# A hybrid encoder layer on one core: norm, sums and transposes behind the last output round given out in steps

## The chip, the cores and the metric

The kernel runs on one core of a Trainium2 chip. The metric is the device time of one execution, in microseconds. The engines are TensorE (PE, with its weight loads shown apart as PEld), VectorE (DVE), ScalarE (ACT), GpSimd (POOL) and SyncE (SP), which issues the transfers.

## The reference

One layer of an encoder trunk on a sequence of 1024 positions with 1024 channels, in float32:

```
h  = RMSNorm(x);  [q|k|v|glu|q_mem] = h @ W_in
A  = dilated sliding-window attention, 8 heads x 64
B  = GLU -> depthwise conv 31 -> LayerNorm -> swish
C  = cross-attention into 256 memory tokens, 4 heads x 64
x  = x + concat(A, B, C) @ W_out
x  = x + ConvFFN(RMSNorm(x))
     ConvFFN: up (1024 -> 2 x 2816) -> depthwise conv 3 -> silu(gate) * up -> down (2816 -> 1024)
```

The change touches what lies between the last two lines: the second RMSNorm, and the way its result gets into the up projection.

## The kernel before

Every matrix product is made in three passes: each operand is split into a high part, rounded to the format that TensorE multiplies quickly, and a low part, the rest, and the products high x high, high x low and low x high are added up. `split` (L1203 on) does it for weights: ScalarE copies the high part (L1207), GpSimd or VectorE subtracts it for the low part (L1208).

The residual lies in eight tiles `x_sb[t]` of 128 positions x 1024 channels. The output projection adds to them in six rounds. In the last round, after the two products of tile t, the generator `norm(t)` is started: `sp.dma_start` stores the row for the end, ScalarE sums the squares, GpSimd makes the inverse root in two instructions (`rsqrt`, L164 and L165), and VectorE scales both halves of the row by it and by the gains (L1173, two instructions).

The up projection isn't made as eight block products, but in the manner of Strassen and Winograd, as seven: the normed rows, transposed, form a two by two block matrix. Its rows of blocks are the tiles 0 to 3 and 4 to 7, its columns the two halves of the channels. The seven left operands are A11, A12 (tiles 0 to 3), A22 (tiles 4 to 7) and the sums S1, S2, S3, S4. For t from 4 on `norm` makes the sums in place, of the rows of tile t and of tile t - 4: `high1` becomes high0 + high1 on GpSimd (L1183), `high0` becomes low0 - high0 on VectorE (L1184), `low0` becomes high1 - low0 on VectorE (L1185), and `low1` becomes low1 - low0 on GpSimd (L1189). `high1` is transposed as A22 before it is overwritten. "Tile 5" below is x_sb[5] with its partner x_sb[1].

`turn_rows` makes one operand's 128 columns: four transposes on TensorE into a PSUM tile `ps_n` (L1159; two buffers, under the tag "turn"), then ScalarE copies the high part out (L1161), then VectorE subtracts for the low part (L1162). `norm` has 24 such turns, two (A11, A12) for each t under 4 and four (A22, S1, S3, S2) for each t from 4 on; four S4 turns follow later. So a turn must wait for a free `ps_n`, which is freed by its second reader.

Then comes the up stage. `first_column` makes the A11 and A12 products of the first two column tiles early, in `ps_a`. `gated(ct)` does one column tile of gate and up (22 rounds): it loads four weight blocks, makes four sums of them t1 to t4 (`comb`, L1221, on VectorE but for the first two rounds), splits seven operands, and runs seven products of 12 matmuls each (128 x 128 by 128 x 512, L1226). The sums of the products are put together as they come: p5 is ScalarE's copy of the S1 product in `ps_c` (L1278); `cu` gets ps_d + p5 on VectorE (L1280, S3 product); u2 is ps_b + p1 (L1283, S2 product); GpSimd adds u2 to the upper half of cu (L1284); the S4 product goes on adding to `ps_c` and L1286 reads it; the A22 product goes on adding to `ps_d` and L1288 reads it. Thus S4 can't start before p5 is read, and A22 not before L1280. Behind them stands the depthwise convolution: ScalarE's scaled copy (L1293) and two VectorE instructions (L1294, L1295) for each of yu and yg, Silu on ScalarE (L1296), and the gate's product (L1297). The down stage (`ps_dn`, L1334) then runs over the stored gate.

The order of the work comes from two places. The program is written with generators: `st.start` hands one over, and each `st.tick()` moves all that are alive by one `yield`; `out_projections` yields after every six matmuls, so that a generator's instructions fall between them. On that written order the framework's scheduler sets the order of each engine's instructions by its own timeline, with priorities. So a change in the written order can change the order of instructions far behind it. Every engine runs its queue strictly in order.

Of the kernel before, what the change touches and what calls it, by code (L numbers as in the profile page):

```python
# [132 lines left out]
def block(tc, a, out):  # L133
# [3 lines left out]
    def f32(ap):  # L137
        return ap.bitcast(F)
# [23 lines left out]
    def rsqrt(dst, src, scale):  # L162

        pool.tensor_scalar(dst, src, scale, EPS, OP.mult, OP.add)  # L164
        pool.tensor_tensor(dst, dst, expo[:, : dst.shape[1]], OP.pow)  # L165
# [989 lines left out]
    def turn_rows(rows, nm, t):  # L1155

        ps = psp.tile([128, KH, 128], F, name="ps_n", tag="turn", bufs=2)
        for k in range(KH):
            pe.transpose(ps[:, k], rows[:, 128 * k : 128 * k + 128], ident)  # L1159
        hi, lo = (x[:, :, 128 * t : 128 * t + 128] for x in ops[nm])  # L1160
        act.activation(hi, ps, AF.Copy)  # L1161
        dve.tensor_tensor(lo, ps, f32(hi), OP.subtract)  # L1162

    def norm(t):
        x = x_sb[t]
        sp.dma_start(h_d[t], x)
        sq = p3r.tile([128, D], F, name="sq2", tag="wide", bufs=2)
        col = ss2[:, t : t + 1]
        act.activation(sq, x, AF.Square, accum_out=col)
        rsqrt(col, col, 1.0 / D)  # L1170
        for i, g in enumerate(g_ffn):
            half = x[:, 512 * i : 512 * i + 512]
            dve.scalar_tensor_tensor(half, half, col, g, OP.mult, OP.mult)  # L1173
        if t < 4:
            turn_rows(x[:, 0:512], "A11", t)
            turn_rows(x[:, 512:1024], "A12", t)
            yield
            return
        yield

        (low0, low1), (high0, high1) = ((y[:, 0:512], y[:, 512:1024]) for y in (x_sb[t - 4], x))
        turn_rows(high1, "A22", t - 4)
        pool.tensor_tensor(high1, high0, high1, OP.add)  # L1183
        dve.tensor_tensor(high0, low0, high0, OP.subtract)  # L1184
        dve.tensor_tensor(low0, high1, low0, OP.subtract)  # L1185
        turn_rows(high1, "S1", t - 4)
        turn_rows(high0, "S3", t - 4)
        turn_rows(low0, "S2", t - 4)
        pool.tensor_tensor(low1, low1, low0, OP.subtract)  # L1189
        yield  # L1190
# [176 lines left out]
```

## Time and profile before

| | us |
|---|---|
| median of 3 runs | 1310.51 (1309.11 to 1313.55) |
| the profiled execution's own time | 1310.28 |
| its span in the trace | 1308.5 |
| mean granted clock of TensorE | 0.963 of full speed |
| busy: TensorE, VectorE, GpSimd, ScalarE | 1197.1, 868.7, 788.5, 626.6 |

About 1.8 us of the profiled time lie outside its span. The stages that matter here: the last round of the output projection with the first products of the up stage ends at about 594.5 us of the span; the transposes go on to about 624.7; the up stage goes on to about 1064, and the down stage to the end. In the lines below a row of an engine's timeline has its start, its duration, engine, line, operation, written tile <- read tiles, shapes, count, and in brackets the idle time before it with what ended it.

### The profile page before, as it was taken

The numbers are of one execution on the slowest core, as the hardware profiler recorded it, in microseconds if no ns is written. First come the engines' busy times: TensorE is split into PE (matmuls) and PEld (weight loads), VectorE is DVE, ScalarE is ACT, GpSimd is POOL, SyncE is SP. The second block draws the span as 40 slices with busy tenths as digits, with TensorE's granted clock in tenths as the row PEclk, the third lists the DMA queues.
The fourth block names the chain that finished last, engine by engine and source line by source line (L and its number), as shares of the span: only waits on it lengthen the run. The fifth ranks groups of instructions, "written<-read, shape, count | busy, mean of one in ns | idle before, by whom it ended". The sixth has DMA issues, their size and how long they took to land.

```text
span 1308.5 us, 18556 instructions
## 1 busy us (share of the span) xinstructions
PE 1197.1 (91%) x6287; PEld 1000.3 (76%) x6287; DVE 868.7 (66%) x1272; ACT 626.6 (48%) x1296; POOL 788.5 (60%) x793
## 2 busy tenths in 40 slices
PE   4899988799988898885999999999999999999997
PEld 3887887799877786563877777777777788888886
DVE  6748879676685786887487778778787762224222
ACT  5664165468766576553344444344444443333331
POOL 4835286498894454367466667676676745555552
PEclk9999988999989898896999999999999999999999
DMA  7353525566575622161122222222222254448443
GB/s 253 112 170 100 159 82 161 169 180 178 144 252 164 188 74 78 28 213 49 34 87 81 65 86 67 81 89 65 89 71 83 81 175 155 145 145 272 146 146 120
DMA packets 166555, 164.81 MB, mean 126 GB/s; under 512 B 20322, under 2 KB 125756, under 8 KB 166460
## 3 DMA queue, kind: packets, MB, share of 16 engines
q1 hardware_dynamic: 166460, 163.63, 40.3%
q8 instruction: 49, 0.80, 0.3%
q14 instruction: 46, 0.38, 0.1%
HBM read 121.51 MB, written 42.08 MB: 125 GB/s over the span
## 4 chain that ended last, share of the span: by engine, by line
PE 46%; DVE 18%; issue 8%; ACT 7%; POOL 6%; DMA 5%; SPq 1%; POOLq 0%; ACTq 0%; DVEq 0%
PE ps_dn L1334 18%; PE ps_c L1226 6%; PE ps_d L1226 6%; PE proj L1099 4%; PE proj L917 3%; DVE yg L1295 3%; DVE conv L980 2%; DVE yu L1295 2%; PE o L287 2%; DMA v<-vr_d 2%; POOL up_lo L1208 2%; PE turn L278 2%; PE ps_a L1226 2%; ACT yu L1293 2%; DVE yg L1294 1%
## 5 line engine op out<-in xcount | busy, mean ns | idle before, releaser
L917 PE MATMUL proj<-w_hi,hnT 128*128 128x256 f32 x896 | 188.1, 298 | 23.7 <-ACT raw L832 12.9
L1208 POOL TENSOR_TENSOR up_lo<-dn_raw,up_hi 128x512 fp32r<-128x512 f32 x88 | 131.7, 1517 | 114.1 <-ACT up_hi L1207 111.3
L1208 POOL TENSOR_TENSOR up_lo<-up_sum,up_hi 128x512 fp32r<-128x512 f32 x88 | 154.8, 1768 | 55.8 <-PE ps_c L1226 22.7
L917 PEld LDWEIGHTS proj<-w_hi,hnT 128*128 128x128 f32 x896 | 150.9, 200 | 27.9 <-ACT raw L832 14.1
L1208 POOL TENSOR_TENSOR up_lo<-up_raw,up_hi 128x512 fp32r<-128x512 f32 x66 | 116.0, 1760 | 68.8 <-PE ps_a L1226 46.3
L1208 DVE TENSOR_TENSOR up_lo<-dn_raw,up_hi 128x512 fp32r<-128x512 f32 x44 | 57.6, 1311 | 147.5 <-ACT up_hi L1207 141.4
L1207 ACT ACTIVATE up_hi<-dn_raw 128x512 fp32r<-128x512 f32 x132 | 75.1, 623 | 161.4 <-issue 118.8
L1334 PE MATMUL ps_dn<-up_lo,up_hi 128*128 128x512 f32 x352 | 136.8, 389 | 0.0
L1334 PE MATMUL ps_dn<-up_hi,up_lo 128*128 128x512 f32 x352 | 136.3, 389 | 0.0
L1334 PE MATMUL ps_dn<-up_hi 128*128 128x512 f32 x352 | 134.7, 389 | 0.0
L917 PE MATMUL proj<-w_lo,hnT 128*128 128x256 f32 x448 | 131.9, 294 | 0.0
L1226 PE MATMUL ps_c<-S,up_hi 128*128 128x512 f32 x352 | 113.5, 404 | 6.6 <-ACT p L1278 6.6
L1226 PE MATMUL ps_a<-A,up_hi 128*128 128x512 f32 x352 | 111.1, 396 | 0.0
L636 POOL TENSOR_TENSOR w_lo<-w_raw,w_hi 128x512 fp32r<-128x512 f32 x44 | 62.8, 1437 | 59.4 <-ACT w_hi L634 58.8
L1221 DVE TENSOR_TENSOR up_sum<-up_raw,up_sum 128x512 f32<-128x512 f32 x40 | 59.0, 1476 | 50.4 <-POOL up_lo L1208 50.4
L917 PEld LDWEIGHTS proj<-w_lo,hnT 128*128 128x128 f32 x448 | 89.7, 200 | 0.5 <-POOL w_lo L624 0.4
L980 DVE SCALAR_TENSOR_TENSOR conv<-conv,cwT 128x1009 f32<-128x1009 f32 (+14 forms) x60 | 89.3, 1488 | 0.8
L1226 PEld LDWEIGHTS ps_c<-S,up_hi 128*128 128x128 f32 x352 | 65.4, 190 | 28.3 <-ACT p L1278 13.6
L1111 DVE TENSOR_TENSOR x<-proj,x 128x512 f32<-128x512 f32 x96 | 64.1, 682 | 25.0 <-PE proj L1099 24.9
L1293 ACT ACTIVATE yu<-cu,fwT 128x1024 f32<-128x1024 f32 x22 | 27.4, 1244 | 108.0 <-DVE cu L1286 106.3
L1226 PEld LDWEIGHTS ps_a<-A,up_hi 128*128 128x128 f32 x352 | 65.8, 188 | 15.8
L1334 PEld LDWEIGHTS ps_dn<-up_lo,up_hi 128*128 128x128 f32 x352 | 66.1, 188 | 13.8
(240 smaller groups left out, 3150.2 us busy)
## 6 DMA issues: line engine op xcount, KB each, us to landing
up_raw<-w_up SPq DMA_DIRECT2D x92, 256.0 KB
dn_raw<-w_down SPq DMA_DIRECT2D x88, 256.0 KB
g_d<-yg SPq DMA_DIRECT2D x22, 512.0 KB
dn_raw<-g_d SPq DMA_DIRECT2D x44, 256.0 KB
x<-x SPq DMA_DIRECT2D x16, 512.0 KB
qk_d<-out SPq DMA_DIRECT2D x32, 256.0 KB
qk<-qk_d SPq DMA_DIRECT2D x16, 512.0 KB
w_raw<-w_in SPq DMA_DIRECT2D x40, 128.0 KB
```

Source lines behind the costliest of these rows:

```text
L636: (dve if next(chunk_no) < EARLY else pool).tensor_tensor(lo, raw, f32(hi), OP.subtract)
L917: pe.matmul(ps[:, :256], lhs[i][:, k], c.parts[k][j], start=(k == 0 and i == 0 and j == 0), stop=(k == KT - 1 and i == 1))
L980: dve.scalar_tensor_tensor(acc[:, c0:c1], conv_in[i][:, c0 + k - 15 : c1 + k - 15], w, acc[:, c0:c1], OP.mult, OP.add)
L1099: pe.matmul(ps, mixed[k][i][:, 128 * t : 128 * t + 128], wo[k, half][j], start=(n == 0), stop=(n == 3 * len(ks) - 1))
L1111: dve.tensor_tensor(dst, ps, dst, OP.add)
L1207: act.activation(hi, src, AF.Copy)
L1208: adder.tensor_tensor(lo, src, f32(hi), OP.subtract)
L1221: adder.tensor_tensor(t, x, y, OP.subtract)
L1226: pe.matmul(ps, w[i][:, k], ops[x][j][:, k], start=(first and n == 0), stop=(n == 3 * KH - 1), skip_group_check=not first)
L1293: act.activation(y, c, AF.Identity, scale=tap[1], bias=b)
L1295: dve.scalar_tensor_tensor(y[:, 0 : S - 1], c[:, 1:S], tap[2], y[:, 0 : S - 1], OP.mult, OP.add)
L1334: pe.matmul(ps, gk[i][:, 128 * t : 128 * t + 128], wk[half][j], start=(k == 0 and m == 0), stop=(k == NF - 1 and m == 2))
```

## The change

In `norm`, `yield`s are added: two after `rsqrt`, three after the scaling, one between the turns of A11 and A12, three after the two VectorE sums, and one behind each of the turns of S1 and S3. One, ahead of the part for t from 4 on, is taken out. A turn of the next tile's products can be written between any two of these steps. No instruction is added or removed.

```
--- before.py
+++ after.py
@@ -1168,23 +1168,31 @@
         col = ss2[:, t : t + 1]
         act.activation(sq, x, AF.Square, accum_out=col)
         rsqrt(col, col, 1.0 / D)
+        for _ in range(2):
+            yield
         for i, g in enumerate(g_ffn):
             half = x[:, 512 * i : 512 * i + 512]
             dve.scalar_tensor_tensor(half, half, col, g, OP.mult, OP.mult)
+        for _ in range(3):
+            yield
         if t < 4:
             turn_rows(x[:, 0:512], "A11", t)
+            yield
             turn_rows(x[:, 512:1024], "A12", t)
             yield
             return
-        yield
 
         (low0, low1), (high0, high1) = ((y[:, 0:512], y[:, 512:1024]) for y in (x_sb[t - 4], x))
         turn_rows(high1, "A22", t - 4)
         pool.tensor_tensor(high1, high0, high1, OP.add)
         dve.tensor_tensor(high0, low0, high0, OP.subtract)
         dve.tensor_tensor(low0, high1, low0, OP.subtract)
+        for _ in range(3):
+            yield
         turn_rows(high1, "S1", t - 4)
+        yield
         turn_rows(high0, "S3", t - 4)
+        yield
         turn_rows(low0, "S2", t - 4)
         pool.tensor_tensor(low1, low1, low0, OP.subtract)
         yield
```

Behind the diff all lines move down by 2 to 8: L1173 is now L1175, L1183 to L1185 are L1187 to L1189, L1189 is L1197, and from L1207 on 8 are added (L1221 is L1229, L1286 is L1294, L1297 is L1305). The order of instructions moves on all engines, from the last output round to the end of the up stage. Three places follow. In the rows x_4988 to x_4995 are the tiles x_sb[0] to x_sb[7], and ss_7000 holds the sums of squares.

GpSimd, from the last inverse root (tile 7) on, before:

```order
L165 TENSOR_TENSOR ss_7000<-ss_7000,expo 128x1
L1189 TENSOR_TENSOR x_4988<-x_4988 128x512
L1208 TENSOR_TENSOR up_lo<-up_sum,up_hi 128x512
L1208 TENSOR_TENSOR up_lo<-up_raw,up_hi 128x512
L1221 TENSOR_TENSOR up_sum<-up_raw 128x512
L1208 TENSOR_TENSOR up_lo<-up_sum,up_hi 128x512
L1221 TENSOR_TENSOR up_sum<-up_raw 128x512
L1221 TENSOR_TENSOR up_sum<-up_raw,up_sum 128x512
L1183 TENSOR_TENSOR x_4993<-x_4993 128x512
L1208 TENSOR_TENSOR up_lo<-up_sum,up_hi 128x512 x2
L1221 TENSOR_TENSOR up_sum<-up_raw,up_sum 128x512
L1208 TENSOR_TENSOR up_lo<-up_sum,up_hi 128x512
```

and after:

```order
L165 TENSOR_TENSOR ss_7000<-ss_7000,expo 128x1
L1187 TENSOR_TENSOR x_4993<-x_4993 128x512
L1197 TENSOR_TENSOR x_4988<-x_4988 128x512
L1216 TENSOR_TENSOR up_lo<-up_sum,up_hi 128x512
L1216 TENSOR_TENSOR up_lo<-up_raw,up_hi 128x512
L1216 TENSOR_TENSOR up_lo<-up_sum,up_hi 128x512
L1229 TENSOR_TENSOR up_sum<-up_raw 128x512 x2
L1197 TENSOR_TENSOR x_4989<-x_4989 128x512
L1187 TENSOR_TENSOR x_4994<-x_4994 128x512
L1229 TENSOR_TENSOR up_sum<-up_raw,up_sum 128x512
L1216 TENSOR_TENSOR up_lo<-up_sum,up_hi 128x512 x2
```

The sum of tile 5 (x_4993) has moved from behind seven instructions to directly behind the inverse root, and the sums of tiles 6 and 7 have come nearer to it, ahead of weight sums and splits that stood before them.

TensorE, from the turn of S2 of tile 4 (it reads x_4988) to the first products of `gated` (ps_d, with the turn of S2 of tile 7, which reads x_4991, and the first S4 turn, which reads x_4988 again, beside them), before:

```order
L1159 MATMUL ps_n<-identr,x_4988 128x128 x4
L1159 MATMUL ps_n<-identr,x_4993 128x128 x12
L1159 MATMUL ps_n<-identr,x_4989 128x128 x4
L1159 MATMUL ps_n<-identr,x_4994 128x128 x12
L1159 MATMUL ps_n<-identr,x_4990 128x128 x4
L1159 MATMUL ps_n<-identr,x_4995 128x128 x12
L1226 MATMUL ps_d<-S_6998,up_hi 128x512 x2
L1159 MATMUL ps_n<-identr,x_4991 128x128 x4
L1159 MATMUL ps_n<-identr,x_4988 128x128 x4
L1226 MATMUL ps_d<-S_6999,up_hi 128x512
```

and after:

```order
L1159 MATMUL ps_n<-identr,x_4994 128x128 x4
L1159 MATMUL ps_n<-identr,x_4988 128x128 x4
L1159 MATMUL ps_n<-identr,x_4993 128x128 x8
L1159 MATMUL ps_n<-identr,x_4995 128x128 x4
L1159 MATMUL ps_n<-identr,x_4989 128x128 x4
L1159 MATMUL ps_n<-identr,x_4994 128x128 x8
L1159 MATMUL ps_n<-identr,x_4990 128x128 x4
L1159 MATMUL ps_n<-identr,x_4995 128x128 x8
L1159 MATMUL ps_n<-identr,x_4991 128x128 x4
L1234 MATMUL ps_d<-S_6998,up_hi 128x512 x2
L1159 MATMUL ps_n<-identr,x_4988 128x128 x4
L1234 MATMUL ps_d<-S_6999,up_hi 128x512
```

Before, the three turns A22, S1 and S3 of a tile stand together (x12). Now A22 of tile 6 comes ahead of S1 of tile 5, and so on; the A22 turn of tile 5 is no longer here, since it stands among the A11 products of `first_column` (17 of them are ahead of it).

VectorE, one round in the middle of the up stage (`up_sum<-up_raw` are t1 and t3, `up_sum<-up_raw,up_sum` t2 and t4), before:

```order
L1280 TENSOR_TENSOR cu<-ps_d,p_9026 128x512
L1221 TENSOR_TENSOR up_sum<-up_raw,up_sum 128x512
L1283 TENSOR_TENSOR u_9027<-ps_b,p_9024 128x512
L1221 TENSOR_TENSOR up_sum<-up_raw,up_sum 128x512
L1286 TENSOR_TENSOR cu<-ps_c,u_9027 128x512
L1294 SCALAR_TENSOR_TENSOR yu<-cu,fwT,yu 128x1023
L1288 TENSOR_TENSOR cg<-ps_d,u_9027 128x512
L1295 SCALAR_TENSOR_TENSOR yu<-cu,fwT,yu 128x1023
L1294 SCALAR_TENSOR_TENSOR yg<-cg,fwT,yg 128x1023
L1295 SCALAR_TENSOR_TENSOR yg<-cg,fwT,yg 128x1023
L1221 TENSOR_TENSOR up_sum<-up_raw 128x512 x2
L1297 TENSOR_TENSOR yg<-yg,yu 128x1024
```

and after:

```order
L1288 TENSOR_TENSOR cu<-ps_d,p_9026 128x512
L1229 TENSOR_TENSOR up_sum<-up_raw,up_sum 128x512
L1291 TENSOR_TENSOR u_9027<-ps_b,p_9024 128x512
L1294 TENSOR_TENSOR cu<-ps_c,u_9027 128x512
L1229 TENSOR_TENSOR up_sum<-up_raw,up_sum 128x512
L1302 SCALAR_TENSOR_TENSOR yu<-cu,fwT,yu 128x1023
L1296 TENSOR_TENSOR cg<-ps_d,u_9027 128x512
L1303 SCALAR_TENSOR_TENSOR yu<-cu,fwT,yu 128x1023
L1302 SCALAR_TENSOR_TENSOR yg<-cg,fwT,yg 128x1023
L1303 SCALAR_TENSOR_TENSOR yg<-cg,fwT,yg 128x1023
L1305 TENSOR_TENSOR yg<-yg,yu 128x1024
L1229 TENSOR_TENSOR up_sum<-up_raw 128x512 x2
```

L1286 (now L1294) has moved ahead of t4, and L1297 (now L1305) ahead of t1 and t3, directly behind L1295 (now L1303). TensorE's products in such a round stand, before, in the order S3, A12, S1, S2, A11 of the round after, S4, A22; now S3, S1, two matmuls of S2, A12, the rest of S2, S4, one matmul of A11 of the round after, A22, the rest of that A11. GpSimd's order within these rounds is the same. On ScalarE Silu is now followed by the split of w1, p5, and the split of w2.

More of the change, by code (lines that the diff above doesn't have):

```diff
@@ L1170, in norm @@
         rsqrt(col, col, 1.0 / D)
+        for _ in range(2):
+            yield
         for i, g in enumerate(g_ffn):
@@ L1173, in norm @@
             dve.scalar_tensor_tensor(half, half, col, g, OP.mult, OP.mult)
+        for _ in range(3):
+            yield
         if t < 4:
             turn_rows(x[:, 0:512], "A11", t)
+            yield
             turn_rows(x[:, 512:1024], "A12", t)
@@ L1178, in norm @@
             return
-        yield
         (low0, low1), (high0, high1) = ((y[:, 0:512], y[:, 512:1024]) for y in (x_sb[t - 4], x))
@@ L1185, in norm @@
         dve.tensor_tensor(low0, high1, low0, OP.subtract)
+        for _ in range(3):
+            yield
         turn_rows(high1, "S1", t - 4)
+        yield
         turn_rows(high0, "S3", t - 4)
+        yield
         turn_rows(low0, "S2", t - 4)
```

## The prediction

> **What bounds the kernel now.** I read the page's shares first, then a table of busy time by stage, then the waits of the two stages that the diff can touch, then the instructions of each engine there.
>
> ```profile
> PE 1197.1 (91%) x6287; PEld 1000.3 (76%) x6287; DVE 868.7 (66%) x1272; ACT 626.6 (48%) x1296; POOL 788.5 (60%) x793
> 594.50:624.70 30.20, 14.72 (x59) 10.79 (x60) 20.33 (x24) 10.14 (x17) 18.62 (x15) 0.56 0.15 44
> 624.70:693.50 68.80, 65.91 (x288) 52.58 (x286) 48.04 (x42) 29.84 (x44) 38.62 (x23) 1.00 0.18 58
> 693.50:754.20 60.70, 60.48 (x251) 47.98 (x251) 47.91 (x39) 26.34 (x40) 41.39 (x26) 0.97 0.25 79
> 754.20:1063.80 309.60, 306.10 (x1284) 238.61 (x1285) 240.19 (x198) 134.18 (x199) 207.31 (x121) 1.00 0.27 85
> 1063.80:1308.50 244.70, 236.94 (x1046) 195.90 (x1044) 73.56 (x63) 72.84 (x127) 125.58 (x84) 0.99 0.49 161
> ```
>
> The columns of a stage are its window and length, then busy time (and count) of PE, PEld, DVE, ACT and POOL, then the granted clock. TensorE is busy for 91% of the span, so only a stage where it idles, or runs under its own pace, has anything to give. The first is 594.5 to 624.7, the stretch of the transposes ("turns"): 14.72 of 30.20 us, at a clock of 0.56. The second hides behind 306.10 of 309.60 us in the up stage: a matmul's modelled end overlaps the next one's start, so pace has to be read from starts. The chain of work that ended last gives them, for the S4 product (12 matmuls into ps_c) of some rounds, and last for the first products of the down stage:
>
> ```profile
> 714.63 2.80 PE ps_c L1226 x12
> 734.23 2.79 PE ps_c L1226 x12
> 754.25 3.07 PE ps_c L1226 x12
> 774.55 3.07 PE ps_c L1226 x12
> 1038.64 3.06 PE ps_c L1226 x12
> 1055.70 2.76 PE ps_dn L1334 x12
> ```
>
> From 714.63 to 734.23 a round of 84 matmuls takes 19.60 us (2.80 for 12: TensorE's own pace). From 754.25 to 1038.64 there are 14 rounds of 20.31 us each. So something else than TensorE sets the rounds there. The waits of 754 to 1064 say what (us in total, times, longest):
>
> ```profile
> ACT yu L1293 <- DVE cu L1286: 89.3, 15, 6.4
> DVE up_sum L1221 <- POOL up_lo L1208: 38.1, 14, 2.7
> DVE yu L1294 <- ACT yu L1293: 20.8, 16, 1.4
> PEld ps_c L1226 <- ACT p L1278: 10.2, 15, 0.7
> PEld ps_d L1226 <- DVE cu L1280: 5.3, 14, 0.4
> ```
>
> TensorE waits briefly twice in each round, for p5 (L1278) and for cu (L1280). The long waits are among the vector engines. One round on VectorE, with the two GpSimd instructions that it waits for:
>
> ```profile
> 1016.06 2.39 DVE L1221 TENSOR_TENSOR up_sum<-up_raw 128x512 f32<-128x512 f32 x2
> 1018.37 2.32 DVE L1297 TENSOR_TENSOR yg<-yg,yu 128x1024 f32<-128x1024 f32 x1
> 1020.61 0.68 DVE L1280 TENSOR_TENSOR cu<-ps_d,p 128x512 f32<-128x512 f32 x1
> 1022.32 0.68 DVE L1283 TENSOR_TENSOR u<-ps_b,p 128x512 f32<-128x512 f32 x1
> 1023.14 1.29 POOL L1284 TENSOR_TENSOR cu<-cu,u 128x512 f32<-128x512 f32 x1 [1.29 <-DVE u L1283]
> 1024.39 1.29 POOL L1208 TENSOR_TENSOR up_lo<-up_sum,up_hi 128x512 fp32r<-128x512 f32 x1
> 1025.72 1.77 DVE L1221 TENSOR_TENSOR up_sum<-up_raw,up_sum 128x512 f32<-128x512 f32 x1 [2.72 <-POOL up_lo L1208]
> 1027.41 0.68 DVE L1286 TENSOR_TENSOR cu<-ps_c,u 128x512 f32<-128x512 f32 x1
> 1029.46 1.28 DVE L1294 SCALAR_TENSOR_TENSOR yu<-cu,fwT,yu 128x1023 f32<-128x1023 f32 x1 [1.38 <-ACT yu L1293]
> 1034.22 2.21 DVE L1295 SCALAR_TENSOR_TENSOR yg<-cg,fwT,yg 128x1023 f32<-128x1023 f32 x1
> 1037.62 1.23 DVE L1297 TENSOR_TENSOR yg<-yg,yu 128x1024 f32<-128x1024 f32 x1 [1.19 <-ACT yg L1296]
> ```
>
> This closes on itself: t1 and t3 at 1016.06, ..., L1283, then GpSimd's L1284 and the low part of w4, then t4 (L1221 at 1025.72, whose buffer that low part was reading), L1286, ScalarE's yu, L1294 to L1295, which ends at 1036.43, when the next round's t1 starts: 20.3 us. L1286 stands behind t4 in VectorE's queue although S4, its input, ended at 1021.4: 6 us lost there, and ScalarE and L1294 wait behind it. The vector loop, not TensorE, is the bound of some 15 rounds.
>
> **The change, part by part.** No instruction is added or removed. Only orders move: in `norm` by the yields, and behind it in the up stage, where the scheduler came out with another order on all engines.
>
> *Turns.* The waits of 545 to 640, with the instructions:
>
> ```profile
> PE ps_n L1159 <- POOL x L1183: 6.8, 2, 5.4
> PE ps_n L1159 <- DVE x L1184: 5.2, 2, 4.5
> 601.51 1.12 PE L1159 MATMUL ps_n<-identr,x 128*128 128x128 f32 x4 [5.42 <-POOL x L1183]
> 607.08 1.09 PE L1159 MATMUL ps_n<-identr,x 128*128 128x128 f32 x4 [4.45 <-DVE x L1184]
> 590.12 0.54 POOL L165 TENSOR_TENSOR ss<-ss,expo 128x1 f32<-128x1 f32 x1
> 600.20 1.26 POOL L1183 TENSOR_TENSOR x<-x 128x512 f32<-128x512 f32 x1
> 601.42 2.53 POOL L1208 TENSOR_TENSOR up_lo<-up_sum,up_hi 128x512 fp32r<-128x512 f32 x2
> 603.90 1.27 POOL L1221 TENSOR_TENSOR up_sum<-up_raw,up_sum 128x512 f32<-128x512 f32 x1
> 605.12 1.27 POOL L1208 TENSOR_TENSOR up_lo<-up_sum,up_hi 128x512 fp32r<-128x512 f32 x1
> 587.10 1.18 DVE L1184 TENSOR_TENSOR x<-x,x 128x512 f32<-128x512 f32 x1
> 601.49 5.44 DVE L1184 TENSOR_TENSOR x<-x,x 128x512 f32<-128x512 f32 x1 [4.04 <-POOL x L1183]
> ```
>
> The sum of tile 5 (L1183) sits on GpSimd at 600.20 behind seven operations for the first weights, and TensorE waits 5.42 us for it. In the new order it stands directly behind L165, so it starts at 590.66: a lead of 9.54 us. Its A22 transposes, which must read the old rows first, go into the A11 products. The turns of neighbouring tiles alternate, so one tile's sums run beside another's turns. What eats the lead is the pair of last rows: the same L1184 takes 1.18 us and, while GpSimd ran four operations in a row, 5.44. A further L1184 starved like that costs 4.26. None gives 9.5 of gain, one 5.3, two 1.0; those are the ends. GpSimd keeps three to six operations in a row behind the sums of tiles 5 and 6, so I take one: **-5.3**.
>
> The Trainium skill, "SBUF — State Buffer", "SBUF: two separate sides", calls the ports that VectorE and GpSimd share an exclusive lock: whichever starts first keeps it for its instruction and the other blocks. The row is harsher: 5.44 us spans all of GpSimd's 2.53 + 1.27 + 1.27, so the loser lost four times over. By the page a blocked L1184 would take one operation more and the gain would be near 9; the row decides.
>
> *Rounds of the up stage.* TensorE's order becomes S3, S1, S2, A12, S4, A22 with A11 of the round after around them. VectorE's moves L1286 ahead of t4 and L1297 directly behind L1295, ahead of t1 and t3. In the loop above that takes away L1286 and the wait for yu (1029.46 less 1027.41: 2.05 us), which now lie beside t4's 1.77. It adds the wait for Silu, which t1 and t3 covered: the row at 1037.62 shows it uncovered, 1.19. So 20.3 - 2.05 + 1.19 = 19.4 us, under TensorE's 19.60: the bound passes to TensorE. From S4's end to the end of the next L1280 I add 0.68 + 1.77 + 6.97 (1029.46 to 1036.43) + 1.19 + 2.32 + 2.39 + 0.68 = 16.0; A22 of the next round starts 19.8 after that S4's end. This lead of nearly 4 us absorbs a loop that is somewhat long: at 20.0, 15 rounds lose 6 and get 4 of it back. p5 stands behind one Silu and one copy on ScalarE, some 4 us ahead of S4 as well. Ends: the loop stays at 20.3 (0), or TensorE's pace everywhere. The latter: 734.23 to 1038.64 is 304.41 us for 15 rounds; 15 x 19.60 = 294.0; **-10.4**, which I take.
>
> *First rounds.* Before 693.5 VectorE is also late once:
>
> ```profile
> PE ps_c L1226 <- ACT p L1278: 2.9, 1, 2.9
> ```
>
> There S4 waits for p5 behind a Silu. In the new order S4 comes 12 matmuls (2.8 us) sooner in its round, the vector work hardly sooner. Between -2.9 (stall gone) and +2.8 (twice as long) I take **+0.5**.
>
> *End of the up stage.* The first 12 products of the down stage stand between the last rounds in both orders (the row at 1055.70, at TensorE's pace), and the last gate (L1297) is stored and loaded again before its use. Bounds -1 and +2.3 (one L1297 late), taken **+0.5**. The down stage (1063.8 on) keeps its order.
>
> Sum: -5.3 - 10.4 + 0.5 + 0.5 = -14.7. The profiled execution took 1310.28 us, 0.23 under the median of the runs (1310.51): **1295.6**, I say 1295.5.
>
> **The rivals.**
> 1. *The vector loop stays the bound.* For it: 19.4 is only 0.2 under 19.60, and L1221 and L1297 cost nearly double beside GpSimd (1.23 against 2.32 for L1297). Against it: the 4 us of lead, and the loop is summed with the dear values. Then only the turns gain: 1310.3 - 5.3 + 1 = 1306.
> 2. *The turns give the lead back, the rounds gain.* Two starved L1184: 1310.3 - 1.0 - 10.4 + 1 = 1300. For it the 5.44; against it that GpSimd itself soon has to wait for VectorE (L1189 needs L1185), which ends any starving.
> 3. *Slower: VectorE blocked behind GpSimd in every round.* Now t4 starts when GpSimd is through; moved behind L1286, it and L1297 may each meet one GpSimd operation more (1.27 each). The loop is then 19.4 + 2.5 = 21.9; 15 rounds lose 2.3 each, less 4 of lead: 30.5 over TensorE's pace where 10.4 are lost now, so 1310.3 + 20.1 - 4.3 = 1326. It decides from a loop of about 21 us, 0.7 over today's. Against it: by the stage's row VectorE is busy 240.19 and GpSimd 207.31 of 309.60 us, 15.8 and 13.6 of a round of 20.3, with much of their waiting for each other counted in it, so both have room in 19.6.
> 4. *Nothing changes*: the lead of the turns is lost and the loop stays: 1310.
>
> **How the numbers follow.** The forecast 0.57, rival 2 0.18, rival 1 0.12, rival 3 0.10, rival 4 0.03. 0.3% is 3.9 us, about what a measurement of this kernel can tell from no change. Faster takes the forecast, rival 2 and half of rival 1 (1306 lies at that edge): 0.81; I say 0.80. Same: the other half and rival 4, 0.09. Slower: rival 3 and a little, 0.11. The forecast's own range is 1289 to 1301 (its turns between 9.5 and 1, first rounds and end between their bounds). The range that holds rivals 1, 2 and 4 and the good end (9.5 + 10.4 + 2.9 = 22.8 under) is 1287 to 1311; it leaves out rival 3.
>
> **What would show it.** Right: S4 to S4 in the chain 19.6 us from about 700 to 1040; no wait of PE for p5 or L1280 in steady rounds; L1294 (now L1302) no longer waiting for yu; VectorE waiting about 1.2 us in each round for Silu; dense products from about 619 instead of 624.7; and no 5.42 wait of ps_n for the sum. Wrong: S4 to S4 still at 20.3 or over, with VectorE's L1221 waiting for GpSimd or L1297 near 3 us; more than one L1184 over 4 us; or a stall over 3 us in the first four rounds.

## The result and the profile after

| | before | after |
|---|---|---|
| median of 6 runs each, us | 1311.87 (1309.11 to 1313.97) | 1296.35 (1292.69 to 1300.54) |
| ratio, with its 95% interval | | 0.9884 [0.9868, 0.9901] |
| span of the profiled execution | 1308.5 | 1290.9 |

The forecast was 1295.5. The two profiles differ by 17.6 us, the ratio is worth 15.2; why the two need not agree stands at the end.

The page of the changed kernel, its busy shares and the chain by engine:

```profile
PE 1190.4 (92%) x6287; PEld 1002.1 (78%) x6287; DVE 829.5 (64%) x1272; ACT 633.0 (49%) x1296; POOL 768.5 (60%) x793
PE 46%; DVE 2%; issue 1%; POOL 0%; DMA 0%; ACT 0%; SPq 0%; POOLq 0%; DVEq 0%; ACTq 0%
```

Two of its stages, the turns and the rounds, with the windows cut where its own stages end:

```profile
594.50:619.00 24.50, 16.89 (x65) 12.31 (x66) 18.78 (x23) 9.09 (x16) 20.70 (x14) 0.58 0.19 54
754.20:1046.00 291.80, 291.80 (x1253) 234.45 (x1252) 198.18 (x192) 139.53 (x196) 178.35 (x117) 1.00 0.27 88
```

TensorE is busy for 16.89 of 24.50 us in the first, still at a clock of 0.58, and for all of the second. VectorE's share of the chain fell from 18% to 2%: no vector instruction stands in the way any more in the rounds. It also has less to do there: over this window the same instructions keep VectorE busy 13.3 us of a round of 19.6 (198.18 of 291.80), where it was 15.8 of 20.3. The chain, S4 of three rounds, the ends of a stretch of 15 rounds among them:

```profile
724.81 2.80 PE ps_c L1234 x12
744.41 2.80 PE ps_c L1234 x12
1018.81 2.80 PE ps_c L1234 x12
```

294.00 us for 15 rounds: 19.60 each. One of the later rounds on VectorE:

```profile
845.25 0.69 DVE L1294 TENSOR_TENSOR cu<-ps_c,u 128x512 f32<-128x512 f32 x1 [2.02 <-PE ps_c L1234]
847.06 0.69 DVE L1229 TENSOR_TENSOR up_sum<-up_raw,up_sum 128x512 f32<-128x512 f32 x1 [1.12 <-POOL up_lo L1216]
847.67 1.28 DVE L1302 SCALAR_TENSOR_TENSOR yu<-cu,fwT,yu 128x1023 f32<-128x1023 f32 x1
855.82 1.23 DVE L1305 TENSOR_TENSOR yg<-yg,yu 128x1024 f32<-128x1024 f32 x1 [1.19 <-ACT yg L1304]
856.97 0.68 DVE L1229 TENSOR_TENSOR up_sum<-up_raw 128x512 f32<-128x512 f32 x1
858.85 0.69 DVE L1229 TENSOR_TENSOR up_sum<-up_raw 128x512 f32<-128x512 f32 x1 [1.20 <-POOL up_lo L1216]
```

And one of the earlier rounds: two S4 sums that follow each other, with t1 and t3 between them, and then the busy times of an earlier and of a later round (the columns are those of the stages above):

```profile
748.01 0.69 DVE L1294 TENSOR_TENSOR cu<-ps_c,u 128x512 f32<-128x512 f32 x1
761.49 3.50 DVE L1229 TENSOR_TENSOR up_sum<-up_raw 128x512 f32<-128x512 f32 x2
767.41 0.69 DVE L1294 TENSOR_TENSOR cu<-ps_c,u 128x512 f32<-128x512 f32 x1
747.28:766.88 19.60, 19.60 (x86) 15.75 (x84) 16.16 (x15) 8.98 (x14) 13.01 (x8) 1.00 0.26 84
845.28:864.88 19.60, 19.60 (x86) 15.75 (x84) 12.65 (x14) 9.32 (x14) 11.97 (x9) 1.00 0.25 81
```

The waits of the whole up stage, 640 to 1046 (us in total, times, longest):

```profile
DVE cu L1294 <- PE ps_c L1234: 27.9, 13, 3.6
PE ps_d L1234 <- DVE cu L1288: 4.4, 2, 3.7
```

The first row of the later round is the change of bound: the S4 sum now waits 2.02 us for TensorE, where it stood behind t4 with its input long ready. This room isn't there from the start. In rounds 4 to 8 the S4 sum doesn't wait for TensorE, and the sums follow each other at 19.40 us (748.01 to 767.41), so VectorE, busy for 16.16 us a round (16.20 in a steady round of before), gains 0.20 on TensorE's 19.60 each time. From round 10 on it waits; it is busy for 12.65 in the later round shown. Silu is uncovered by 1.19 us, as foreseen, and costs nothing. TensorE waits in the up stage only twice, in rounds 2 and 3 (3.7 and 0.7 us). In the turns (545 to 640) the waits for GpSimd's sums are gone, and many short ones for the low parts took their place (the waits again, before and after):

```profile
PE ps_n L1159 <- DVE S L1162: 1.3, 3, 0.8
PE ps_n L1159 <- DVE S L1162: 8.7, 9, 2.2
```

The first S3 product starts at 613.80, where it was 621.81:

```profile
613.80 1.20 PE L1234 MATMUL ps_d<-S,up_hi 128*128 128x512 f32 x2
```

Landmarks that both kernels share, from the starts of TensorE's instructions in the two profiles, give where the 17.6 us come from. The changed order has 11 matmuls of A11 (2.57 us) behind A22 that stood ahead of it; the two rows at A22 are set right for that.

| stretch | before | after | difference | forecast |
|---|---|---|---|---|
| start to the last A12 product of `first_column` | 594.07 | 592.96 | -1.1 | 0 |
| to the first S3 product (the turns) | 27.74 | 20.84 | -6.9 | -5.3 |
| to A22 of round 4 (first rounds) | 95.5 | 94.3 + 2.6 | +1.4 | +0.5 |
| to A22 of round 20 (16 rounds) | 324.3 | 313.6 | -10.7 | -10.4 |
| to the end | 266.96 | 269.24 - 2.57 | -0.3 | +0.5 |

### The profile page after: what moved, and what is told of

Same layout as the page of the kernel before. It is cut to its first block, busy times and chain, and to the rows that moved or that the text cites. A ratio compares the mean times of both kernels' runs of the same rounds, so it can differ in the third digit from the quotient of the medians.

```text
span 1290.9 us, 18539 instructions
## 1 busy us (share of the span) xinstructions
PE 1190.4 (92%) x6287; PEld 1002.1 (78%) x6287; DVE 829.5 (64%) x1272; ACT 633.0 (49%) x1296; POOL 768.5 (60%) x793
## 5 line engine op out<-in xcount | busy, mean ns | idle before, releaser
L1216 POOL TENSOR_TENSOR up_lo<-up_sum,up_hi 128x512 fp32r<-128x512 f32 x88 | 142.5, 1624 | 55.6 <-ACT up_hi L1215 48.6
L1216 POOL TENSOR_TENSOR up_lo<-up_raw,up_hi 128x512 fp32r<-128x512 f32 x66 | 103.7, 1573 | 89.5 <-ACT up_hi L1215 79.0
L1234 PE MATMUL ps_a<-A,up_hi 128*128 128x512 f32 x352 | 114.2, 396 | 0.0
L1234 PE MATMUL ps_c<-S,up_hi 128*128 128x512 f32 x352 | 110.4, 395 | 0.0
L1215 ACT ACTIVATE up_hi<-up_sum 128x512 fp32r<-128x512 f32 x88 | 55.0, 628 | 89.9 <-PE ps_c L1234 43.9
L1342 PEld LDWEIGHTS ps_dn<-up_hi,up_lo 128*128 128x128 f32 x352 | 66.1, 188 | 13.9
L1342 PEld LDWEIGHTS ps_dn<-up_hi 128*128 128x128 f32 x352 | 66.1, 188 | 13.7
```

The lines of the kernel that those rows point to most:

```text
L1215: act.activation(hi, src, AF.Copy)
L1216: adder.tensor_tensor(lo, src, f32(hi), OP.subtract)
L1234: pe.matmul(ps, w[i][:, k], ops[x][j][:, k], start=(first and n == 0), stop=(n == 3 * KH - 1), skip_group_check=not first)
L1342: pe.matmul(ps, gk[i][:, 128 * t : 128 * t + 128], wk[half][j], start=(k == 0 and m == 0), stop=(k == NF - 1 and m == 2))
```

## The experiments

Theory A: two gains that have nothing to do with each other on the chip: shorter turns, and rounds that pass from the vector loop to TensorE because the S4 sum no longer stands behind t4. Its rivals are in the expectations. In the diffs, `behind(key, make)` issues what `make` makes on VectorE behind the recorded instruction `key`, in the queue's order alone; nothing waits for its end. "Stretch" is the one of the table's second row. Each ratio is to the kernel before in the same batch of runs; the medians of before lie between 1311.87 and 1315.62 us, so between batches the ratios count and not the times. In the rows of a pinned kernel the lines are moved again; the tiles tell which is which: `cu<-ps_c` is the S4 sum, "DVE cu L1288" the S3 sum.

**One edit alone.**

```
 # before
         dve.tensor_tensor(low0, high1, low0, OP.subtract)
+        for _ in range(3):
+            yield
         turn_rows(high1, "S1", t - 4)
```

> The kernel before with one of the edits alone: the three yields behind the two VectorE sums of norm. Built, its instructions stand on all engines almost as in the changed kernel (4 of 5297 rows of TensorE differ, 6 of 1141 of VectorE, none of GpSimd), while the kernel with all the other yields and without these three stands as before. Theory A (the time hangs on the two new orders: GpSimd's sum of tile 5 directly behind the inverse root, and VectorE's order in the rounds): 1296 us, the changed kernel's time. Rival (each added yield brings its share, by letting other work in between): a third to a half of the 15 us, 1303 to 1306.

Measured 1298.52 us, ratio 0.9878 [0.984, 0.9916]; stretch 20.86, rounds 19.60, the same two waits in rounds 2 and 3. These three yields are the whole change; on the chip the other edits are worth nothing that can be seen.

**The rounds, with norm untouched.** Three kernels pin VectorE's order in the rounds and leave the turns as they were.

```
 # t4 alone
-        t4 = comb(b21, t2, adder)
+        t4 = behind(("cu", ct - 2), lambda: comb(b21, t2, adder))   # "cu": L1286
 # t1 and t3 alone
-        t1 = comb(b12, b11, adder)
+        t1 = behind(("gate", ct - 3), lambda: comb(b12, b11, adder))   # "gate": L1297
-        t3 = comb(b22, b12, adder)
+        t3 = behind(("gate", ct - 3), lambda: comb(b22, b12, adder))
 # both: all three lines
```

> The kernel before, norm untouched; in the up stage t4 of a round is pinned behind the S4 sum (L1286) of the round two ahead, as in the changed kernel. VectorE's t1 and t3 stay ahead of the gate's product, TensorE keeps the order of before (S3, A12, S1, S2, A11, S4, A22). Theory A (L1286 behind t4 is what makes the vector loop longer than TensorE's round): the loop falls from 20.3 to 18.3, TensorE's 19.6 takes over: S4 to S4 19.60, 10 us less, 1301. Rival B (TensorE's new order, S4 directly behind S2, makes the rounds short, VectorE's order only follows): rounds stay at 20.3, 1311.

> The kernel before, norm untouched; only t1 and t3 of a round are pinned behind the gate's product (L1297), so that VectorE has nothing to do while ScalarE makes Silu; t4 stays ahead of the S4 sum. Theory A: the loop grows by Silu's 1.2 us to 21.5, S4 to S4 21.5, some 15 rounds: +18 us, 1329. Rival B (TensorE's order sets the rounds): 20.3 and 1311.

> The kernel before, norm untouched, with both pins of the two runs above: VectorE's order in the rounds is that of the changed kernel, TensorE's order and the turns are those of before. Theory A: loop 20.3 - 2.05 + 1.2 = 19.4, under 19.6: S4 to S4 19.60, 1301, as with t4 alone. Rival B: 20.3, 1311. Rival C (the loop of 19.4 has no room beside GpSimd, and only TensorE's new order gives VectorE the lead that it needs): between, about 20, 1306.

Measured: t4 alone 1304.32 us, ratio 0.9932 [0.9911, 0.9952]; t1 and t3 alone 1326.06, 1.0085 [1.0055, 1.0115]; both 1308.14, 0.996 [0.9943, 0.9977]. The rounds with t4 alone, by the products into ps_d in the chain (A22 and S3, 24 in a row):

```profile
819.93 5.60 PE ps_d L1226 x24
839.53 5.60 PE ps_d L1226 x24
```

VectorE's S4 sum in the same run:

```profile
839.57 0.69 DVE L1294 TENSOR_TENSOR cu<-ps_c,u 128x512 f32<-128x512 f32 x1 [4.44 <-PE ps_c L1226]
```

With t1 and t3 alone, the starts of A22 on TensorE, then VectorE behind Silu:

```profile
826.21 0.73 PE L1226 MATMUL ps_d<-A,up_hi 128*128 128x512 f32 x2 [1.23 <-DVE cu L1288]
847.34 0.73 PE L1226 MATMUL ps_d<-A,up_hi 128*128 128x512 f32 x2 [1.23 <-DVE cu L1288]
842.02 1.23 DVE L1305 TENSOR_TENSOR yg<-yg,yu 128x1024 f32<-128x1024 f32 x1 [1.19 <-ACT yg L1304]
843.16 3.52 DVE L1221 TENSOR_TENSOR up_sum<-up_raw 128x512 f32<-128x512 f32 x2
```

With both, A22 in the chain:

```profile
823.22 3.08 PE ps_d L1226 x12
843.15 3.08 PE ps_d L1226 x12
```

And t4, then t1 and t3, on VectorE in that run:

```profile
847.05 1.78 DVE L1221 TENSOR_TENSOR up_sum<-up_raw,up_sum 128x512 f32<-128x512 f32 x1 [1.96 <-POOL up_lo L1208]
858.91 3.51 DVE L1221 TENSOR_TENSOR up_sum<-up_raw 128x512 f32<-128x512 f32 x2
```

One instruction moved on VectorE, with TensorE's old order, gives 19.60, and VectorE then waits 4.4 us in every round from round 5 on: rival B (TensorE's order makes the rounds short) falls. The kernel gains less than the rounds do, since its first rounds take 98.9 us (from the first S3 product to A22 of round 4) for 95.5. Moving t1 and t3 alone makes the rounds 21.13 and the kernel slower, so this half of the new order is a loss in itself. It is 0.8 more, where 1.2 was expected: Silu's 1.19 is there, but the gate's product is shorter (1.23 for 2.32), and t2 too (0.67 for 1.18), while t1 and t3 together are longer (3.52 for 2.39). With both, 19.93: not the 19.4 of my sum, and a third of a microsecond over TensorE's pace. Rival C was right for this one.

**TensorE's order on top of both.** The pins above, and the matmuls of the rounds held in the changed kernel's order (A11 and S3 from round 5 on). ScalarE's order in the rounds, not pinned, followed into the changed kernel's as well.

```
 # both pins, and
+    for i in a12: tc.add_manual_dep(i, s2[1].name, ...)        # A12 behind two of S2
+    for i in s2[2:]: tc.add_manual_dep(i, a12[-1].name, ...)
+    tc.add_manual_dep(a11[0], last["S4", ct - 1].name, ...)     # one of A11 behind S4
+    for i in a11[1:]: tc.add_manual_dep(i, last["A22", ct - 1].name, ...)
+    for i in s3: tc.add_manual_dep(i, a11[-1].name, ...)
```

> The kernel with both vector pins (rounds of 19.92 us), and TensorE's order in the rounds pinned besides as in the changed kernel: A12 between the second and third matmul of S2, one A11 matmul between S4 and A22, the other eleven behind A22, S3 behind them. Norm and the turns as before. Theory C (with t1 and t3 behind the gate the loop only fits if TensorE's new order frees the weights' buffers one by one, so that GpSimd's splits are spread and don't meet VectorE's t1 and t3): 19.60, 5 us less than with the two pins alone, 1303. Rival (what is missing lies in ScalarE's or GpSimd's order, or in the turns): 19.9, 1308.

Measured 1308.09 us, ratio 0.9943 [0.9915, 0.9972], the interval too wide to tell it from the run with both. The rounds tell it, by the starts of A22 and by t4, and t1 and t3, on VectorE:

```profile
821.31 0.63 PE L1227 MATMUL ps_d<-A,up_hi 128*128 128x512 f32 x2
840.91 0.63 PE L1227 MATMUL ps_d<-A,up_hi 128*128 128x512 f32 x2
843.81 0.69 DVE L1221 TENSOR_TENSOR up_sum<-up_raw,up_sum 128x512 f32<-128x512 f32 x1 [1.95 <-POOL up_lo L1208]
854.65 3.51 DVE L1221 TENSOR_TENSOR up_sum<-up_raw 128x512 f32<-128x512 f32 x2
```

19.60, so TensorE's order, with ScalarE's, is what the two vector pins lack; which of the two does it isn't told apart, so the part of the rival that names ScalarE stands. The reason that I gave isn't shown: t4 is short now (0.69 for 1.78), but t1 and t3 are as long as with the two pins (3.51), and t2 is longer (1.38 for 0.67). The first rounds lost 2.4 us more here (waits of 1.75 and 3.52 for the S3 sum) and the turns 1.5 (an L1184 of 5.43 us, below), which hides the gain in the total.

**The turns.** First GpSimd's place alone (before, no yields), then the reverse: the changed kernel with that place undone.

```
 # before: L1189 of tile 4, and the lows and sums of the first weights, queued behind the sum of tile 5
+        tc.add_manual_dep(lows[4], sums[5].name, ...)
+        with tc.issue_after(sums[5]): ...        # w2, w22, w4 of round 0; all of round 1
 # after: the sum of tile 5 queued behind t2 of round 1 (vector order of the rounds pinned)
+        tc.add_manual_dep(sums[5], t2_of_round_1.name, ...)
```

> The kernel before without any added yield; only GpSimd's sum of tile 5 (L1183) is pinned directly behind the inverse root, ahead of the seven operations for the first weights. TensorE keeps the turns tile by tile, A22 of tile 5 behind the first products, and the scheduler by itself then gives the rounds the changed kernel's order. The stretch from the first turn behind the A12 products to the first S3 product was 25.4 us in the runs with norm untouched (27.0 in the profile of before) and 18.7 in the changed kernel. Theory A1 (GpSimd's place is what counts): the sum starts when A22 of tile 5 is through, some 4 us sooner than now, so the stretch is 21 to 22, rounds 19.6, total about 1300. Rival A2 (the alternating turns carry the gain, the place of the sum nothing): 25.4, 1303.

> The changed kernel with GpSimd's sum of tile 5 pinned back behind the weight sums and splits of the first two rounds; TensorE's turns alternate as in the changed kernel. VectorE's order in the rounds is pinned as in the changed kernel, since the scheduler would otherwise fall back to that of before; TensorE's order in the rounds is that of before. Theory A1: the turn of S1 of tile 5 waits for the sum at about 10 us into the stretch; 25 us or more for the stretch. Rival A2: the other tiles' turns fill the wait, 19 to 20 us. Rounds as in the run with both pins, 19.9 by that run: total 1308 by A1, 1302 by A2.

Measured: sum early 1303.37 us, ratio 0.992 [0.989, 0.9951], stretch 27.95, rounds 19.60; sum late 1305.44, ratio 0.9936 [0.9913, 0.9958], stretch 25.19, rounds 19.89. TensorE's turns with the sum early:

```profile
600.86 0.66 PE L1159 MATMUL ps_n<-identr,x 128*128 128x128 f32 x4 [1.41 <-POOL x L1185]
611.63 1.11 PE L1159 MATMUL ps_n<-identr,x 128*128 128x128 f32 x4 [4.72 <-POOL x L1185]
617.17 1.09 PE L1159 MATMUL ps_n<-identr,x 128*128 128x128 f32 x4 [4.43 <-DVE x L1188]
```

GpSimd's sum of tile 5 and VectorE's first difference of tile 6 in the same run (L1185 and L1188 are L1183 and L1184 of before):

```profile
599.53 1.27 POOL L1185 TENSOR_TENSOR x<-x 128x512 f32<-128x512 f32 x1 [4.71 <-PE ps_n L1159]
611.61 5.42 DVE L1188 TENSOR_TENSOR x<-x,x 128x512 f32<-128x512 f32 x1 [3.34 <-POOL x L1185]
```

The longest wait with the sum late:

```profile
602.61 1.11 PE L1159 MATMUL ps_n<-identr,x 128*128 128x128 f32 x4 [6.51 <-POOL x L1189]
```

A1 falls for the first: the wait of 5.42 us for tile 5 shrank to 1.41, and 4.72 and 4.43 came back at tile 6. In TensorE's old order the sum of tile 5 waits 4.71 us for its A22 turn, though it is first in GpSimd's queue, and the weight operations behind it are pushed late: GpSimd works without a pause from 599.5 to 616.5, tile 6's sum comes in the middle of that, and one L1188 takes 5.42. A2 falls for the second: with alternating turns and a late sum TensorE stands 6.51 us. Neither half gains much (27.95 and 25.19 for 27.74); only both together give 20.84.

**The turns alone.** t1 and t3 of round 2 pinned behind the last S2 turn of the changed kernel; the scheduler then falls back to the old order in the rounds.

```
 # after
-        t1 = comb(b12, b11, adder)
+        t1 = behind(("norm", ct), lambda: comb(b12, b11, adder))   # "norm", 2: L1162 of the last S2 turn
 # t3 likewise
```

> The changed kernel with t1 and t3 of round 2 pinned behind the last turn of norm. The turns and GpSimd's sums are those of the changed kernel, but with this pin the scheduler gives the rounds the order of before on TensorE and VectorE (t4 ahead of the S4 sum). Theory A (two separate gains): stretch of the turns 20.8 us or a little less, S4 to S4 20.3: 1305 to 1306. Rival E (the earlier start alone lets the rounds run at TensorE's pace): 19.6 and 1296.

Measured 1302.08 us, ratio 0.9891 [0.9852, 0.9929]; stretch 19.95; S4 of two rounds in the chain:

```profile
823.30 3.06 PE ps_c L1236 x12
843.63 3.06 PE ps_c L1236 x12
```

20.33: an earlier start of the up stage doesn't cure the rounds, and rival E falls. Against the before of its own batch (1315.62) the total is 13.5 us less, some 7 more than expected, since the first rounds gained as well: 89.8 us from the first S3 product to A22 of round 4, for 95.5 before. So this kernel, with the old rounds, has about the ratio of the changed one. That the pin itself shortens the first rounds, because it takes t1 and t3 of round 2 out of the way of the turns, is likely but wasn't tried apart.

**Towards a faster one.** The first rounds' last waits, and then the parts put together.

```
 # after: rounds 4 and 5 behind the S3 sums of rounds 2 and 3
+        t1 = behind(("high", ct - 2) if ct in (4, 5) ..., ...)   # "high": L1280; t3 likewise
 # the turns alone, and t4 behind L1286
 # all pins: that, and the two lines above
```

> The changed kernel with one pin more, in the first rounds: t1 and t3 of rounds 4 and 5 go behind the S3 sums (L1280, now L1288) of rounds 2 and 3, for which the A22 products wait 3.74 and 0.65 us in the changed kernel. Theory A (an order of two instructions costs that wait; VectorE has room soon after): both waits go, 4.4 us less, 1292. Rival D (VectorE is full in these rounds, the wait only moves to the next S4 or A22): 1296, and a wait of like size by 700 us.

> The kernel of the run above with the pin of t4 behind the S4 sum of the round two ahead added, so VectorE's t1 and t3 keep hiding Silu and TensorE keeps its order of before. Theory A: stretch 20 to 21, rounds 19.60, first rounds as in the run with t4 alone (waits of 1.5 and 2.9): 1295, with the changed kernel or 1 to 2 us under it. Rival F (the pin at the turns costs the first rounds what it saves): 1298.

> The kernel with the changed kernel's turns, t1 and t3 of round 2 behind the last turn, and t4 behind the S4 sum; and besides t1 and t3 of rounds 4 and 5 behind the S3 sums of rounds 2 and 3, for the last two waits of TensorE in its first rounds (1.18 for L1288, 0.66 for p5). Theory A: rounds 19.60, the waits gone or moved as in the run with that pin alone (which gained 0.9): 1293, a ratio to before of 0.983 with a tighter interval, under the changed kernel's 0.988. Rival D (VectorE is full there, the wait moves and grows): 1296 and 0.986.

Measured: 1294.31 us, ratio 0.9852 [0.9816, 0.9888]; 1294.13, 0.9831 [0.9793, 0.9869]; 1290.97, 0.983 [0.9799, 0.9861]. In the first the waits of 3.74 and 0.65 became 1.49 (L1288) and 2.07 (p1 on ScalarE): rival D, with 0.8 gained. The second has the stretch at 19.96, the first rounds at 92.9 and the rounds at 19.60. The third's interval lies just under the changed kernel's 0.9868 to 0.9901. It keeps the good half of the new vector order (t4) and leaves out the other. Against the second its first rounds (91.6) are 1.3 shorter, which the two intervals can't tell apart.

**A second profile of before.**

> The kernel before once more, for a second profile. VectorE's first L1184 behind the A12 products took 5.44 us in the first profile and 1.75 to 1.76 in the three runs with norm untouched. If that is an accident of the moment at which it meets GpSimd's row of operations: 1.8 here and a stretch of 26.2 from the last A12 product to the first S3 product. If it belongs to this program: 5.4 and 27.7.

VectorE's L1184 of tile 5 in this second profile:

```profile
608.94 5.45 DVE L1184 TENSOR_TENSOR x<-x,x 128x512 f32<-128x512 f32 x1 [4.06 <-POOL x L1183]
```

The same instruction in the run with t4 alone:

```profile
604.15 1.76 DVE L1184 TENSOR_TENSOR x<-x,x 128x512 f32<-128x512 f32 x1 [4.04 <-POOL x L1183]
```

5.45 again, and 5.43 in the run with TensorE's order pinned; 1.75 and 1.76 in the three with the vector pins. Those have the same instructions around it. So it takes one of two values, about 5.4 and about 1.76, and the stretch follows with 27.7 to 27.8 or 26.2 to 26.3. What chooses isn't settled: twice of two in before, but both values with norm untouched.

## Why the prediction was right, step by step

*The bound.* Right: the vector loop was closed over t4 and the S4 sum, and that one swap opens it (t4 alone: 19.60).

*Rounds, -10.4.* Right, -10.7 (over 16 rounds). The loop of 19.4 is what the chip ran in rounds 4 to 8 (19.40), and the margin of 0.2 against TensorE's 19.60 is what VectorE gained there in each. That the size is so exact is in part luck: t1 and t3 took 3.50 for the 2.39 of the sum, the gate's product 1.23 for 2.32, and the two cancel. The lead of nearly 4 us, from the end of the S3 sum to the A22 that waits for it, was 0.9 to 1.7 in those rounds and 4.7 from round 10 on. What the sum didn't foresee is that second state, in which t1 to t4 take 0.69 each. And it holds only with the changed kernel's order on TensorE and ScalarE: with the old one the same vector order gives 19.93.

*Turns, -5.3.* Right in sign, -6.9 measured, within its ends (-9.5, -1.0). The lead is there: the sum of tile 5 starts 3.8 us ahead of the last A12 product, where it started 6.1 behind it. The step that failed is to take this lead, less one starved L1184, as the gain. In the changed kernel no L1188 was starved (1.77, 1.33, 1.16), so by that step the gain should have been 9.5, and more, since the stretch of before already holds a starved one, which the sum doesn't give back; where L1184 took 1.76 in the kernel with t4 alone the stretch was 26.3, not 27.7. What the runs show in its place: the waits for the sums and differences, 12.0 us in the prediction's two rows, are gone, but those for the low parts, by which a turn gets a free `ps_n`, rose from 1.3 to 8.7. The run with the sum early shows that an early place in GpSimd's queue gives nothing by itself: the A22 turn has to come early too.

*The rule on the shared ports.* Where L1184 took 1.76 it was held up by one operation (604.09 to 605.36 in the kernel with t4 alone), as the Trainium skill ("SBUF — State Buffer", "SBUF: two separate sides") has it; where it took 5.4 it was not. The rule's sum, a gain near 9, was no better than mine.

*First rounds, +0.5.* +1.4, within its bounds: the wait of 2.9 became two of 3.74 and 0.65, for L1288 and not for p5. A stall over 3 us in the first four rounds was one of the prediction's signs of being wrong; it came, and cost little because the old stall went. *End, +0.5.* -0.3. *The range.* 1289 to 1301 isn't what the bounds of the terms add up to; with the rounds at -10.4 they give 1286.5 to 1304. The measured 1296.35 lies in both.

*Rivals.* Slower by blocking (rival 3) did not come. Its case, t4 long behind the S4 sum, is nearest to both pins with the old order of TensorE, and that loop is 19.93, not 21.9; t1 and t3 alone, which is slower (21.13 a round), has t4 in its old place and loses by the uncovered Silu. Rival 1's rounds of 20.3 with the new turns were run as the turns alone: a ratio of 0.9891, where 1306 would be 0.997, but 5.7 us of that come from shorter first rounds, which the changed kernel doesn't have.

## What to carry to other kernels

Where an engine works a loop of its own beside TensorE, read the pace of rounds from starts and look for the instruction whose input is long ready while it stands behind one that waits for a third engine: moving that one instruction can be the whole gain of the rounds. A change in written order far ahead can flip the order of a steady state behind it; compare the orders there first, and pin the good one, since it may come in one package with a bad half. Price such a move by running each half: sums from the old kernel's rows carry its collisions.

## What had not been expected of the hardware

TensorE's instructions up to the last product of the output projection stand in the same order in all 14 profiles taken for this case, yet this product starts anywhere from 577.55 to 589.43 us. That is more than any single step measured here; the two profiles of before alone have it at 582.02 and 589.43. It is why differences of 1 to 3 us are read from landmarks inside one trace and not from totals.

What a vector instruction costs beside GpSimd is not settled by the order of the instructions. In the changed kernel the same instructions in the same order keep VectorE busy for 16.16 us of an earlier round and for 12.65 of a later one, both of 19.60; t1 and t3 take 3.50 together in the first and 0.68 and 0.69 in the second. The run with the sum early has the same orders on all engines in the rounds, and stays at about 16.16 to round 18; its rounds are 19.60 as well. The long t1 starts at 761.49, inside a GpSimd instruction (760.97 to 762.74); the short one starts at 856.97 together with one, and the short t3 at 858.85, just behind its end. Why one kernel comes out of the first state and the other doesn't is open.
